# A transformer block's operations recorded first and given out by the kernel's own planner

## The chip, the core and the metric

The kernel runs on one core of one Trainium2 chip. The metric is the device time of one execution in microseconds. TensorE (PE) multiplies, VectorE (DVE) and ScalarE (ACT) work on elements, SyncE (SP) issues most loads, and GpSimd (POOL) issues loads that add into their destination. Each of these engines has a queue of its own; work is handed over between engines by semaphores.

## The reference

One layer of a streaming encoder on 256 tokens with 2048 features, all in float32:

```python
x = x + 0.5 * swiglu(rms_norm(x, ffn1_norm), ffn1_w_up, ffn1_w_down)       # 2048 -> 2 x 5632 -> 2048
proj = rms_norm(x, mix_norm) @ w_in                                        # q, f, i, g, x_b, gate_b, gates
y_a = rms_norm(hgrn2_chunked(q, f, i, lb), hgrn_norm) * silu(g)            # 8 heads of 128
y_b = rglru_branch(x_b, gate_b, conv_w, conv_b, lru_wa, ...)               # conv(4), gates, linear scan, gelu
x = x + (sigmoid(gate_a) * (y_a @ w_branch_a) + sigmoid(gate_b) * (y_b @ w_branch_b)) @ w_out
x = x + cross_attention(rms_norm(x, xattn_norm), rms_norm(mem, mem_norm), wq, wkv, wo)   # 4 heads, 256 memory tokens
x = x + 0.5 * swiglu(rms_norm(x, ffn2_norm), ffn2_w_up, ffn2_w_down)
return rms_norm(x, final_norm)
```

HGRN2 is a gated linear recurrence per head, S_t = diag(f_t) S_(t-1) + (1 - f_t) v_t, read out with q_t. RG-LRU is a first-order recurrence per feature.

## The kernel before

The weights, some 450 MB, are read once, in tiles of 1 MB (128 partitions x 2048). Each tile goes through the same stages: SyncE loads it into `raw` (3 buffers); ScalarE copies it to `h`, rounded to the format TensorE takes (3 buffers); VectorE subtracts `h` from `raw` and leaves the rest in `l` (3 buffers); TensorE multiplies with `h` and `l`, and adds the products in PSUM, which has 8 banks of 128x512. `split` (lines 120 and 121) makes `h` and `l`. The activations are kept as a high and a low part too, so that one product takes three matmuls: high by high, low by high, high by low.

The feed-forward blocks go over 11 groups of 512 hidden columns. A group takes 8 tiles of the gate and up weights; the tiles are "plain", "mixed" or "fast". A fast tile goes through seven instead of eight products, for which VectorE forms four differences first (`td`, lines 213 to 215) and splits them too (`th`, `tl`). For some mixed tiles ("added") the low part is made by a load of GpSimd that adds into `l`. After a group the hidden values are transposed (line 491), and tiles of the down weights follow. `three` (lines 451 to 454) issues the matmuls of one tile. The temporary tiles `td`, `tl`, `ev` and `junk` share a pool `wide` of three buffers.

The mixer and the attention go over their tiles by `product` (lines 231 and 235: weights stationary) or `rows_product` (lines 252 to 255: activations stationary). The recurrences run beside them: `hgrn` and `lru` are generators that stand in a list `side`, and `pump(2)` takes up to two steps of them after each tile. A step of HGRN is some small matmuls on TensorE (lines 768 and 788, tiles of 32 or 16 columns), then a few products on VectorE.

A list `plan` holds all weight tiles in the order of use; `weights` prepares each of them up to two ahead of its use. The program text fixes a priority, and the framework's own scheduler puts the instructions of each engine in order from that priority and from durations of its own. The kernel overrules it at four places: SyncE, ScalarE and VectorE keep the written order for the first eight tiles; the rows' norm, the LRU parameters and the side work are held behind an operation of the main work by `issue_after`.

Of the kernel before, what the change touches and what calls it, by code (L numbers as in the profile page):

```python
# [2 lines left out]

# [4 lines left out]

F32 = mybir.dt.float32
F32R = mybir.dt.float32r  # L10
ACT = mybir.ActivationFunctionType
ALU = mybir.AluOpType
# [45 lines left out]
    return out + [("down", NG - 2, 2, c, b) for c in range(4) for b in (NG - 2, NG - 1)]  # L58


@with_exitstack
def block_kernel(ctx: ExitStack, tc: tile.TileContext, xT, xin, memT, vec, gfin, bgate, lruw, wu1, wd1, win, wv,
                 wg, wab, wout, wq, wk, wvm, wo, wu2, wd2, out_):
    nc = tc.nc
    pe, dve, act, sp = nc.tensor, nc.vector, nc.scalar, nc.sync

    def pool(name, bufs, **kw):
        return ctx.enter_context(tc.tile_pool(name=name, bufs=bufs, **kw))

    const = pool("const", 1)  # L70
    rawp = pool("raw", 3)
# [5 lines left out]
    scoped = {}  # L77

    @contextmanager
    def scope(**pools):  # L80
        with ExitStack() as inner:
            for name, bufs in pools.items():
                scoped[name] = inner.enter_context(tc.tile_pool(name=name, bufs=bufs, reuse_waits="tile"))
            yield
            scoped.clear()

    def slot(dt=F32, name="slot"):
        return slots.tile([P, 1024], dt, name=name, tag="slot")
# [71 lines left out]

    head, rest = [], {}
    planned = count()
    in_turn = ExitStack()

    def weights(*key):
        while plan and len(ahead) < 2:
            i = next(planned)
            k, src, kind = plan.pop(0)
            if i == 0:
                in_turn.enter_context(tc.manual_schedule(engines={sp.engine, act.engine, dve.engine}))  # L170
            if i < len(head):
                head[i]()
            if plan and plan[0][2] == "added":
                begun.append(begin_added(plan[0][1]))
            ahead.append((k, prepare(src, kind, 4 if i < 4 else 1)))
# [10 lines left out]
    def begin_added(src):  # L186

        raw = scoped["own"].tile([P, 2048], F32, name="own", tag="own")
        l = lp.tile([P, 2048], F32R, name="l", tag="l")
        sp.dma_start(raw, src)  # L190
        act.activation(l, raw, ACT.Copy, scale=-1.0)
        nc.gpsimd.dma_start(l, raw, accum_op=ALU.add)
        return raw, l

    def prepare(src, kind, cuts=1):
# [271 lines left out]
    def ffn(name, pairs, sq, then, begin=(), sums=(), rstds=()):  # L467
# [3 lines left out]
        order = orders[name]  # L471
# [7 lines left out]
        rstd = None  # L479
# [26 lines left out]

        for at, e in enumerate(order):
            w = weights(name, *e)
            kind = e[0]
            following = order[at + 1][0] if at + 1 < len(order) else None  # L510
            if kind != "down":
                g, p = e[1:]
                fast = kind == "fast"
                products = []
                for i, (a, b, n) in enumerate(PRODUCTS[kind]):
                    u = uses[g, n]
                    if u[0] == (p, i):
                        accs[n] = bank()
                    own, less = pairs[p]
                    products.append((accs[n], part(own, a, P) if a >= 0 else part(less, -1 - a, P), part(w[b // 4] if fast else w, b % 4, 512),  # L520
                                     u[0] == (p, i), u[-1] == (p, i)))
                three(products)
                last = at + 1 == len(order) or order[at + 1][1] != g or following == "down"
                ends = kind != "plain" and uses[g, 0][-1][0] == p
                if ends or last:
                    if ends or kind == "plain":
                        ev = scoped["wide"].tile([P, 2048], F32, name="ev", tag="wide")
                        e0, e1, e2, e3 = (ev[:, i * 512:(i + 1) * 512] for i in range(4))
                        if rstds:
                            rstd = rstds[0]  # L530
                        if rstd is None:
                            with tc.issue_after(done["high"]):
                                rstd = sq.rstd_tokens()
                if ends:
                    act.activation(e0, accs[0], ACT.Copy)
                    dve.tensor_tensor(out=e1, in0=accs[5], in1=e0, op=ALU.add)
                    dve.tensor_tensor(out=e2, in0=accs[4], in1=e1, op=ALU.add)
                if last:
                    if kind == "plain":
                        activate(e0, accs[0], accs[1], 0)  # L540
                        activate(e3, accs[3], accs[2], 1)
                    else:
                        for o, n, x in ((e0, 1, e0), (e1, 3, e1), (e1, 2, e1)):
                            dve.tensor_tensor(out=o, in0=accs[n], in1=x, op=ALU.add)
                        activate(e0, e0, e1, 0)
                        for o, n, x in ((e3, 6, e2), (e2, 3, e2)):
                            dve.tensor_tensor(out=o, in0=accs[n], in1=x, op=ALU.add)
                        activate(e3, e3, e2, 1)
                    late.append((4 if g else 2, lambda g=g, hid=(e0, e3): turn(g, hid)))
            else:  # L550
                first, n, c, block = e[1:]
                if block == first:
                    accs["down"] = [bank(), bank()]
                for t in range(2):
                    products = []
                    for k in range(4):
                        a = hids[2 * block + k // 2][:, k % 2 * 512:][:, :512]
                        products.append((accs["down"][t], (a[:, t * P:][:, :P], a[:, T + t * P:][:, :P]),
                                         part(w, k, 512), block == first and k == 0, block == first + n - 1 and k == 3))
                    three(products)  # L560
                    if block == first + n - 1:
                        o = xt[c][:, t * 512:(t + 1) * 512]
                        done["residual"] = dve.scalar_tensor_tensor(out=o, in0=accs["down"][t], scalar=0.5, in1=o,
                                                                    op0=ALU.mult, op1=ALU.add).ins
                        if block == NG - 1:
# [84 lines left out]
    def to_mix(c, t):  # L650
        sq2.add(c, [t])
        if t == 0:
            return
        if c == 0:
            with tc.issue_after(done["residual"]):
                parameters()
        if c == 2:
            root_ready(xt[c])
        if c < 3:
            normed(xs2, c, "mix_norm")  # L660
        else:
            late2.append(lambda: normed(xs2, c, "mix_norm"))
# [23 lines left out]
    v = [scoped["extra"].tile([P, 1024], F32, name=f"v{t}", tag="extra") for t in range(2)]  # L686
# [65 lines left out]
    def hgrn(hf):  # L752
        q, f = Q[hf], F[hf]
# [3 lines left out]
        S = scoped["scores"].tile([P, 3 * 512], F32, name="S", tag="S")  # L757
# [16 lines left out]
        nc.gpsimd.memset(S[:, :1024], 0.0)  # L774
        yield
        dve.tensor_tensor(out=q, in0=q, in1=f, op=ALU.mult)
        yield True
# [2 lines left out]
        for li, n in enumerate(LEVELS):  # L780
            acc = bank()
            if n >= 32:
                for g in range(2):
                    for h in range(4):
                        i = g * 4 + h
                        for a in range(0, P, 2 * n):
                            s = g * P + a
                            pe.matmul(acc[a:a + n, i * n:(i + 1) * n], kv[:, h, s:s + n], qv[:, h, s + n:s + 2 * n],
                                      start=True, stop=True)
# [18 lines left out]
            for t, side_of, by in ((q, 1, 0), (kk, 0, 1)):  # L808
                o = t.rearrange("p (j two n) -> p j two n", two=2, n=n)[:, :, side_of]
# [13 lines left out]
        for pair in range(2):  # L823
            os, squares = [], []
            for z in range(2):
                h = pair * 2 + z
                c = (hf * 4 + h) * P
                o = bank()
# [3 lines left out]
                s = t1("osq")  # L832
# [197 lines left out]
    for g in range(4):  # L1030
# [65 lines left out]

    with scope(**FFN_POOLS):
        ffn("ffn2", pairs2, sq4, to_out, late, sums2)


def _layout(inputs):
# [90 lines left out]
```

## Time and profile before

| what | us |
|---|---|
| time, median of the runs (2442.12 to 2442.47) | 2442.3 |
| time of the profiled execution | 2442.24 |
| its span, from the first to the last instruction | 2440.5 |
| TensorE busy | 2430.0 |
| weight loads of TensorE, beside its matmuls | 2033.8 |
| VectorE busy | 1892.8 |
| ScalarE busy | 1390.8 |
| GpSimd busy | 28.3 |

The span begins with the first instruction of the program and ends with its last. A matmul's record ends some time after the next one has begun, so TensorE's busy time is the union of overlapping records. Idle time of an engine is put down to what ended it. The core read 472.07 MB at 194 GB/s over the span, and TensorE's granted clock was 0.999 of full speed.

### The profile page before, as it was taken

Reading aid. Unit: us, or ns where it says so; the run is one execution under the profiler, and the core shown is the slowest. Engines: PE = TensorE matmul, PEld = TensorE weight load, DVE = VectorE, ACT = ScalarE, POOL = GpSimd, SP = SyncE. Lnnn points to the kernel's source line nnn. Section 1 sums busy time; section 2 is a strip of 40 time slices with the busy share of each in tenths; the row PEclk is TensorE's granted clock in tenths of the full one; section 3 lists DMA queues with packets and bytes.
Section 4 is the critical chain, followed back from the end, with each engine's and each line's share of the span. In section 5 each row is a group of like instructions: output and inputs, shape, how many; then the busy total and the mean of one; then the engine's idle time right before and its main releaser. Section 6 shows DMA issues by size and latency. Waiting matters only on the chain.

```text
span 2440.5 us, 30183 instructions
## 1 busy us (share of the span) xinstructions
PE 2430.0 (100%) x12250; PEld 2033.8 (83%) x12250; DVE 1892.8 (78%) x2016; ACT 1390.8 (57%) x1398; POOL 28.3 (1%) x36
## 2 busy tenths in 40 slices
PE   9999999999999999999999999999999999999998
PEld 8888888888888888888888888888888888888887
DVE  6999999999765757577565676556589999999995
ACT  8566666666554454477435554555555666666664
POOL 0000000000000000000000000000000000000000
PEclk9999999999999999999999999999999999999999
DMA  8557777677555545445555555544555677777763
GB/s 296 207 204 243 255 234 236 234 241 239 200 181 192 180 173 179 176 171 217 191 189 186 206 196 190 190 173 155 189 191 185 232 238 234 234 239 241 237 216 151
DMA packets 75020, 507.59 MB, mean 208 GB/s; under 512 B 8320, under 2 KB 8576, under 8 KB 15232
## 3 DMA queue, kind: packets, MB, share of 16 engines
q1 hardware_dynamic: 69840, 473.06, 53.3%
q0 software_dynamic: 4320, 31.46, 6.7%
q8 instruction: 96, 1.57, 0.2%
q10 hardware_dynamic: 720, 1.13, 0.1%
q14 instruction: 44, 0.36, 0.0%
HBM read 472.07 MB, written 2.10 MB: 194 GB/s over the span
## 4 chain that ended last, share of the span: by engine, by line
PE 97%; DVE 1%; ACT 1%; DMA 1%; issue 0%; SPq 0%; ACTq 0%; DVEq 0%
PE acc L451 18%; PE acc L454 18%; PE acc L452 18%; PE acc L231 11%; PE acc L252 8%; PE acc L253 8%; PE acc L255 8%; PE acc L235 6%; PE acc L491 1%; PE acc L391 1%; ACT h L120 0%; PE acc L768 0%; DVE l L121 0%; DMA xf<-xT 0%; PE acc L1051 0%; PE acc L1006 0%
## 5 line engine op out<-in xcount | busy, mean ns | idle before, releaser
L121 DVE TENSOR_TENSOR l<-raw,h 128x2048 fp32r<-128x2048 f32 (+2 forms) x422 | 877.9, 2087 | 364.8 <-ACT h L120 354.7
L120 ACT ACTIVATE h<-raw 128x2048 fp32r<-128x2048 f32 (+2 forms) x422 | 736.7, 1752 | 615.1 <-PE acc L253 206.2
L451 PE MATMUL acc<-h,xh 128*128 128x512 f32 x1280 | 499.0, 391 | 0.4 <-ACT h L120 0.3
L452 PE MATMUL acc<-h,xl 128*128 128x512 f32 x1280 | 496.9, 389 | 0.0
L120 ACT ACTIVATE h<-td 128x1024 fp32r<-128x1024 f32 x224 | 229.7, 1056 | 177.0 <-PE acc L452 130.8
L252 PE MATMUL acc<-h,ops 128*128 128x512 f32 x832 | 326.9, 393 | 0.0
L253 PE MATMUL acc<-h,ops 128*128 128x512 f32 x832 | 324.3, 390 | 0.0
L121 DVE TENSOR_TENSOR tl<-td,h 128x1024 fp32r<-128x1024 f32 x224 | 267.4, 1220 | 31.6 <-ACT h L120 29.0
L451 PEld LDWEIGHTS acc<-h,xh 128*128 128x128 f32 x1280 | 240.3, 188 | 53.2 <-ACT h L120 3.4
L452 PEld LDWEIGHTS acc<-h,xl 128*128 128x128 f32 x1280 | 240.3, 188 | 49.4
L231 PE MATMUL acc<-ops,h 128*128 128x512 f32 x1152 | 277.9, 393 | 0.2
L451 PE MATMUL acc<-h,hidop 128*128 128x512 f32 x704 | 275.7, 392 | 0.0
L452 PE MATMUL acc<-h,hidop 128*128 128x512 f32 x704 | 274.3, 390 | 0.0
L231 PEld LDWEIGHTS acc<-ops,h 128*128 128x128 f32 x1152 | 211.9, 188 | 42.8 <-DVE ops L292 0.9
L454 PE MATMUL acc<-l,xh 128*128 128x512 f32 x832 | 218.3, 389 | 0.0
L255 PE MATMUL acc<-l,ops 128*128 128x512 f32 x832 | 206.1, 390 | 0.0
L454 PE MATMUL acc<-l,hidop 128*128 128x512 f32 x704 | 188.3, 389 | 0.0
L255 PEld LDWEIGHTS acc<-l,ops 128*128 128x128 f32 x832 | 156.2, 188 | 32.4
L454 PEld LDWEIGHTS acc<-l,xh 128*128 128x128 f32 x832 | 156.0, 188 | 32.5
L252 PEld LDWEIGHTS acc<-h,ops 128*128 128x128 f32 x832 | 156.3, 188 | 32.3
L253 PEld LDWEIGHTS acc<-h,ops 128*128 128x128 f32 x832 | 156.3, 188 | 31.6
L454 PEld LDWEIGHTS acc<-l,hidop 128*128 128x128 f32 x704 | 132.2, 188 | 27.5
(220 smaller groups left out, 2347.9 us busy)
## 6 DMA issues: line engine op xcount, KB each, us to landing
raw<-wu SPq DMA_DIRECT2D x142, 1024.0 KB, 4.8
raw<-wd SPq DMA_DIRECT2D x88, 1024.0 KB, 4.8
raw<-win SPq DMA_DIRECT2D x40, 1024.0 KB, 4.8
raw<-wg SPq DMA_DIRECT2D x32, 1024.0 KB, 4.8
own<-wu SPq DMA_DIRECT2D x30, 1024.0 KB, 5.4
l<-own POOLq DMA_DIRECT2D x30, 1024.0 KB, 7.7
raw<-wab SPq DMA_DIRECT2D x16, 1024.0 KB, 4.8
raw<-wout SPq DMA_DIRECT2D x16, 1024.0 KB, 4.8
```

Of the source, the lines that this page charges most:

```text
L120: done["high"] = act.activation(h, raw, ACT.Copy).ins
L121: dve.tensor_tensor(out=l, in0=raw, in1=h.bitcast(F32), op=ALU.subtract)
L231: pe.matmul(acc, h[:, k * P:(k + 1) * P], xs[k], start=k == 0, stop=False)
L235: done["product"] = pe.matmul(acc[:, :T], l[:, k * P:(k + 1) * P], xs[k][:, :T], start=False, stop=k == KT - 1).ins
L252: pe.matmul(accs[t], x[:, t * P:][:, :P], h[j], start=first and j == 0, stop=False)
L253: pe.matmul(accs[t], x[:, T + t * P:][:, :P], h[j], start=False, stop=False)
L255: done["product"] = pe.matmul(accs[t], x[:, t * P:][:, :P], l[j], start=False, stop=last and j == 3).ins
L391: pe.transpose(accs[m // 2][:, m % 2 * T + t * P:][:, :P], tile[:, t * 512 + m * P:][:, :P], ident)
L451: pe.matmul(acc, ah, bh, start=start, stop=False)
L452: pe.matmul(acc, al, bh, start=False, stop=False)
L454: pe.matmul(acc, ah, bl, start=False, stop=stop)
L491: pe.transpose(acc[:, z * T + t * P:][:, :P], hid[t][:, (2 * y + z) * P:][:, :P], ident)
```

## The change

The functions of the kernel no longer call the engines. They call stand-ins that record each operation with its tiles; the body of the kernel, its loops and the operations stay as they are. At the end `flow.emit()` works out an order for all engines in a simulated run with durations that are written in the kernel, and issues every operation in that order, under a mode in which the framework keeps the given order on all engines. The four places that overruled the framework's scheduler are gone.

- `record` notes for every operation whom it must follow: the writer of what it reads, and readers and writers of what it overwrites. PSUM is tracked by bank, other tiles by 32 columns.
- `price` gives it a duration by engine and columns: a matmul 0.0134 us plus a 2400th of a microsecond per column above 128 columns, fixed values below, VectorE 1.042 ns a column plus 0.07 us, ScalarE 0.838 ns a column plus 0.095 us, a load 2.9 us per MB plus 1.9 us.
- `nominal` gives it a place in time: the sum of TensorE's durations recorded before it.
- `aims` gives it a due time: for TensorE its nominal time, for the others the earliest due time of what follows less its own duration and a lag; a successor can pull a TensorE operation earlier too.
- `arrange` runs the engines event by event: a free engine takes, among the operations that are ready, the one with the earliest due time. Nothing runs whose nominal time lies more than 30 us ahead of TensorE. `Ring` hands out buffers: with up to 8 of them in the recorded order alone, with 24 also out of order while more than six are free. It is done three times, since the due times take up which buffers follow one another.
- `emit` names every buffer's place and issues.

```diff
+class Ring:
...
+        self.spare = bufs if bufs <= 8 else bufs // 4
...
+    def when(self, op):
+
+        if not self.free or self.takers[self.head] is not op and len(self.free) <= self.spare:
+            return 1e18
+        return min(self.free)[0]
...
+LAG = {"PE": 0.24, "DVE": 0.15, "ACT": 0.16, "POOL": 0.16, "SP": 0.1}
+AHEAD, BACKLOG = 30, 3
+TABLES = {ACT.Silu, ACT.Sigmoid, ACT.Sqrt, ACT.Exp, ACT.Gelu_apprx_tanh}
...
+    def price(self, op):
+        q, kw = op.queue.name, op.kw
+        n = op.out.cells.size if op.out is not None else 0
+        op.table, op.moved, op.busy = None, 0, 0.0
+        if op.method == "dma_start":
+            v = op.out if op.out is not None else op.args[1]
+            op.moved = v.cells.size * 512 / 2 ** 20 * (5.2 if "accum_op" in kw else 2.9)
+            op.busy = 0.9 if q == "POOL" else 0.06
+        elif q == "PE":
+            op.busy = n / 2400 + 0.0134 if n > 128 else 0.108 if n == 128 else 0.058 if n == 64 else 0.04
+        elif q == "DVE":
+            n = max(n, kw["in_"].cells.size) if op.method == "tensor_reduce" else n
+            per = {"reciprocal": 6.2, "tensor_tensor_scan": 2.2}.get(op.method, 1.042)
+            op.busy = n * per / 1000 + 0.07
+        elif q == "ACT":
+            op.busy = n * 0.838e-3 + 0.095 + (0.1 if "accum_out" in kw else 0)
+            op.table = op.args[2] if op.args[2] in TABLES else None
...
+    def nominal(self):
+        t = 0.0
+        for op in self.ops:
+            op.nominal = t
+            if op.queue.name == "PE":
+                t += op.busy
+
+    def aims(self, order):
+        for op in self.ops:
+            op.due = op.nominal if op.queue.name == "PE" or not op.after else 1e9
+        for op in reversed(order):
+            for s in op.after:
+                lag = op.spent if op.deps is not None and s.deps.get(op, True) is not None else 0
+                op.due = min(op.due, s.due - lag)
...
+            best, soon = None, 1e18
+            for op in cand[e]:
+                r = op.ready
+                if op.scope is not None and any(live[:op.scope]) and any(x.ring.pool.scope is not None for x in op.takes):
+                    continue
+                for x in op.takes:
+                    r = max(r, x.ring.when(op))
+                if op.nominal > reached + AHEAD:
+                    r = 1e18
+                if op.moved:
+                    r = max(r, dma - BACKLOG)
+                if r <= t + 1e-9:
+                    if best is None or op.due < best.due:
+                        best = op
+                else:
+                    soon = min(soon, r)
...
+            if op.table is not None and op.table != table:
+                table = op.table
+                busy += 1.3
...
+        self.nominal()
+        for _ in range(3):
+            self.arrange()
...
+            outer.enter_context(tc.manual_schedule())
+            for op in self.sequence:
...
+                for x in op.takes:
+                    x.at = x.ring.pool.at.tile(x.shape, x.dt, name=x.name, tag=f"{x.ring.tag}{x.index}")
+                getattr(op.queue.real, op.method)(*map(real, op.args), **{k: real(v) for k, v in op.kw.items()})
...
+    flow = Flow(tc)
+    pe, dve, act, sp, gps = flow.queues
+    pool = flow.pool
...
-            if i == 0:
-                in_turn.enter_context(tc.manual_schedule(engines={sp.engine, act.engine, dve.engine}))
...
-            if i == 7:
-                in_turn.close()
...
-                            with tc.issue_after(done["high"]):
-                                rstd = sq.rstd_tokens()
+                            rstd = sq.rstd_tokens()
...
-            with tc.issue_after(done["residual"]):
-                parameters()
+            parameters()
...
-                with tc.issue_after(done["product"]):
-                    n -= n if next(side[0]) else 1
+                n -= n if next(side[0]) else 1
...
+    flow.emit()
```

More of the change, by code (lines that the diff above doesn't have):

```diff
@@ L2 @@
 from itertools import count
+import numpy as np
 import concourse.bass as bass
@@ L6 @@
 from concourse import mybir
-from concourse._compat import with_exitstack
 F32 = mybir.dt.float32
@@ L58, in ffn_order, with __init__, then, __getitem__ @@
     return out + [("down", NG - 2, 2, c, b) for c in range(4) for b in (NG - 2, NG - 1)]
-@with_exitstack
-def block_kernel(ctx: ExitStack, tc: tile.TileContext, xT, xin, memT, vec, gfin, bgate, lruw, wu1, wd1, win, wv,
+class View:
+    def __init__(self, tile, cells, steps=()):
+        self.tile, self.cells, self.steps = tile, cells, steps
+    def then(self, cells, f):
+        return View(self.tile, cells, self.steps + (f,))
+    def __getitem__(self, key):
+        key = key if isinstance(key, tuple) else (key,)
+        return self.then(self.cells[key[1:]], lambda v: v[key if len(key) > 1 else key[0]])
+    def rearrange(self, pattern, **sizes):
+        names = pattern.split("(")[1].split(")")[0].split()
+        return self.then(self.cells.reshape([sizes.get(n, -1) for n in names]),
+                         lambda v: v.rearrange(pattern, **sizes))
+    def bitcast(self, dt):
+        return self.then(self.cells, lambda v: v.bitcast(dt))
+    def broadcast_to(self, shape):
+        return self.then(np.broadcast_to(self.cells, shape[1:]), lambda v: v.broadcast_to(shape))
+    def real(self):
+        v = self.tile.at
+        for f in self.steps:
+            v = f(v)
+        return v
@@ new lines, with __init__, reset, take @@
+class Buffer(View):
+    def __init__(self, ring, shape, dt, name):
+        grain = shape[1] if "space" in ring.pool.kw else 1 if shape[1] <= 128 else 32
+        super().__init__(self, np.arange(shape[1]) // grain)
+        self.ring, self.shape, self.dt, self.name = ring, shape, dt, name
+        self.at = self.index = None
+        n = -(-shape[1] // grain)
+        self.writer, self.readers = [None] * n, [set() for _ in range(n)]
+        self.users = []
+        self.left = 0
+class Ring:
+    def __init__(self, pool, tag, bufs):
+        self.pool, self.tag, self.bufs = pool, tag, bufs
+        self.takers = []
+        self.spare = bufs if bufs <= 8 else bufs // 4
+        self.reset()
+    def reset(self):
+        self.free = [(0.0, i, None) for i in range(self.bufs)]
+        self.head, self.taken = 0, set()
+    def when(self, op):
+        if not self.free or self.takers[self.head] is not op and len(self.free) <= self.spare:
+            return 1e18
+        return min(self.free)[0]
+    def take(self, op):
+        f = min(self.free)
+        self.free.remove(f)
+        self.taken.add(op)
+        while self.head < len(self.takers) and self.takers[self.head] in self.taken:
+            self.head += 1
+        return f
@@ new lines, with __init__, tile @@
+class Pool:
+    def __init__(self, flow, name, bufs, scope, **kw):
+        self.flow, self.name, self.bufs, self.scope, self.kw = flow, name, bufs, scope, kw
+        self.rings = {}
+        self.at = None
+    def tile(self, shape, dt, name, tag=None, bufs=None):
+        tag = tag or name
+        if tag not in self.rings:
+            self.rings[tag] = Ring(self, tag, bufs or self.bufs)
+        return Buffer(self.rings[tag], shape, dt, name)
+class Op:
+    def __init__(self, i, queue, method, args, kw):
+        self.i, self.queue, self.method, self.args, self.kw = i, queue, method, args, kw
+        self.deps, self.after, self.takes, self.frees = {}, [], [], []
+        self.ins = self
+        self.scope = None
@@ L63, in block_kernel @@
+def block_kernel(tc: tile.TileContext, xT, xin, memT, vec, gfin, bgate, lruw, wu1, wd1, win, wv,
                  wg, wab, wout, wq, wk, wvm, wo, wu2, wd2, out_):
[L64 to L68, printed above, removed]
+    flow = Flow(tc)
+    pe, dve, act, sp, gps = flow.queues
+    pool = flow.pool
     const = pool("const", 1)
@@ L80, in scope @@
     def scope(**pools):
[L81 to L85, printed above, removed]
+        for name, bufs in pools.items():
+            scoped[name] = pool(name, bufs, flow.scopes)
+        flow.scopes += 1
+        yield
+        scoped.clear()
     def slot(dt=F32, name="slot"):
@@ L162, in block_kernel @@
     planned = count()
-    in_turn = ExitStack()
     def weights(*key):
@@ L191, in begin_added @@
         act.activation(l, raw, ACT.Copy, scale=-1.0)
-        nc.gpsimd.dma_start(l, raw, accum_op=ALU.add)
+        gps.dma_start(l, raw, accum_op=ALU.add)
         return raw, l
@@ L773, in hgrn @@
                           in1=col("eye", 0, 32)[:, None, :].broadcast_to([P, 8, 32]), op=ALU.mult)
-        nc.gpsimd.memset(S[:, :1024], 0.0)
+        gps.memset(S[:, :1024], 0.0)
         yield
```

181 lines of the change are left out of this document (added).

## The prediction

> **What bounds the kernel now.** I read the page's busy times and its chain first, then who TensorE waited for.
>
> ```profile
> span 2440.5 us, 30183 instructions
> PE 2430.0 (100%) x12250; PEld 2033.8 (83%) x12250; DVE 1892.8 (78%) x2016; ACT 1390.8 (57%) x1398; POOL 28.3 (1%) x36
> PE 97%; DVE 1%; ACT 1%; DMA 1%; issue 0%; SPq 0%; ACTq 0%; DVEq 0%
> PE warm L109 <- DVE ones L106: 1.1, 1, 1.1
> PE acc L451 <- ACT h L120: 0.3, 1, 0.3
> ```
>
> TensorE is the bound from end to end: the chain is 97% its own work, and the only wait in the body that the profile shows is one of 0.3 us. A busy share near 100% still hides small losses, because one matmul's record overlaps the next. So I looked at when matmuls start. The next rows are the timeline: start, duration, instruction. The first real matmul, the two rough places of the ramp, one insertion of small work, and the last matmuls:
>
> ```profile
> 6.99 0.48 PE L451 MATMUL acc<-h,xh 128*128 128x512 f32 x1
> ...
> 27.73 1.29 PE L454 MATMUL acc<-l,xh 128*128 128x512 f32 x5
> 29.31 0.50 PE L451 MATMUL acc<-h,xh 128*128 128x512 f32 x1 [0.28 <-ACT h L120]
> 29.65 0.39 PE L452 MATMUL acc<-h,xl 128*128 128x512 f32 x1
> 29.88 0.40 PE L451 MATMUL acc<-h,xh 128*128 128x512 f32 x1
> ...
> 74.01 0.39 PE L452 MATMUL acc<-h,xl 128*128 128x512 f32 x1
> 74.40 0.50 PE L451 MATMUL acc<-h,xh 128*128 128x512 f32 x1
> 74.74 0.40 PE L452 MATMUL acc<-h,xl 128*128 128x512 f32 x1
> ...
> 76.14 0.64 PE L454 MATMUL acc<-tl,xh 128*128 128x512 f32 x2
> 76.92 0.50 PE L451 MATMUL acc<-h,xh 128*128 128x512 f32 x1
> 77.25 0.40 PE L452 MATMUL acc<-h,xl 128*128 128x512 f32 x1
> ...
> 845.51 1.07 PE L255 MATMUL acc<-l,ops 128*128 128x512 f32 x4
> 846.51 0.74 PE L768 MATMUL acc<-silu,k 128*32 128x16 f32 x64
> 847.18 0.50 PE L252 MATMUL acc<-h,ops 128*128 128x512 f32 x1
> 847.51 0.40 PE L253 MATMUL acc<-h,ops 128*128 128x512 f32 x1
> ...
> 2430.67 1.07 PE L454 MATMUL acc<-l,hidop 128*128 128x512 f32 x4
> ```
>
> From 29.65 to 29.88 a 128x512 matmul takes 0.23 us of the stream. Against that pace the first rough place loses 29.31 - (27.73 + 5 x 0.23) = 0.4 us and 0.1 after it; the second 0.16 + 0.11; the third 0.32 + 0.10. Together 1.2 us. An insertion of HGRN's small matmuls loses about 0.1 going in, 0.1 in its own last step and 0.1 coming out (847.18 to 847.51 is 0.33): 0.3 us. The program makes 28 such insertions (12 for L768, 4 for L788, 2 for L819, 4 for L829, 4 for L838, 2 for L872), which makes 28 x 0.3 = 8.4 us, an estimate. Everything an order can win is in these few microseconds and in the two ends: 6.99 us before the first real matmul, 2440.5 - 2431.7 = 8.8 us after the last.
>
> Then the stretches, which say how much room the other engines have (busy us of TensorE, of its weight loads, VectorE, ScalarE and GpSimd, each with its instructions in brackets; clock, share and GB/s of the transfers), then when the mixer's first product starts on the chain, and who waited for whom:
>
> ```profile
> 6.00:80.00 74.00, 73.58 (x328) 59.03 (x328) 59.99 (x86) 57.34 (x87) 0.00 (x0) 1.00 0.74 272
> 80.00:200.00 120.00, 120.00 (x537) 98.89 (x536) 118.44 (x120) 70.81 (x60) 1.00 (x1) 1.00 0.61 221
> 200.00:600.00 400.00, 400.00 (x1795) 331.81 (x1794) 371.05 (x361) 247.30 (x200) 11.28 (x13) 1.00 0.73 237
> 702.00:1120.00 418.00, 417.88 (x2961) 357.55 (x2960) 269.02 (x313) 222.57 (x238) 1.91 (x2) 1.00 0.51 183
> 1790.00:2420.00 630.00, 630.00 (x2822) 521.92 (x2821) 572.17 (x543) 375.83 (x308) 13.01 (x15) 1.00 0.67 224
> ...
> 702.88 2.72 PE acc L231 x12
> ...
> DVE l L121 <- ACT h L120: 354.7, 222, 4.6
> ACT h L120 <- PE acc L452: 298.9, 194, 3.9
> ACT h L120 <- PE acc L253: 206.2, 70, 4.4
> ```
>
> VectorE (the third busy time) is nearly as full as TensorE in both feed-forward blocks (371 of 400 us, 118 of 120) and has a third of its time free in the mixer. Where it idles, it waits for ScalarE's high halves, and ScalarE waits for TensorE to give a buffer of h back (298.9 + 206.2 us): the producers run ahead until the three buffers are full. That is the slack a new order works with.
>
> **The change part by part.** The profiled execution took 2442.24 us, its span and 1.8 us around it; the median of the runs is 2442.3, so the sum needs no shift.
>
> TensorE's order: for TensorE a due time is the operation's place in the recorded order, unless a successor pulls it earlier. The recording follows the old program text, rings of up to 8 buffers (all 8 PSUM banks, h, l, raw) are given out in recorded order, and matmuls into one bank are chained. So the products keep their order; what can move is small work: the transposes and HGRN/LRU pieces go in when they are ready by the planner's clock, perhaps in the middle of a product. The trace of before has no split piece; bounds are 28 x 0.3 = 8.4 us more if each is cut in two, and 4.2 us less if half of them merge. I take three more cuts, +0.9: most pieces wait for one producer, only LRU's four blocks become ready one by one.
>
> The start: ScalarE runs two small operations of the LRU parameters before the first operand.
>
> ```profile
> 4.31 0.21 ACT L631 ACTIVATE par<-vt 128x8 f32<-128x8 f32 x1 [1.63 <-DMA vt<-vec]
> 4.55 0.21 ACT L632 ACTIVATE par<-par 128x8 f32<-128x8 f32 x1
> 4.66 0.89 ACT L414 ACTIVATE xg<-xf,vt 128x256 f32<-128x256 f32 x2
> 5.59 0.63 ACT L120 ACTIVATE xh<-xg 128x512 fp32r<-128x512 f32 x1
> 6.12 2.45 ACT L120 ACTIVATE h<-raw 128x512 fp32r<-128x512 f32 x4
> 6.86 2.49 DVE L121 TENSOR_TENSOR l<-raw,h 128x512 fp32r<-128x512 f32 x4
> ```
>
> They are recorded at the end of the first feed-forward block, and the planner holds back all that lies over 30 us ahead. They leave the start, and xg can begin at 4.31 instead of 4.66: up to 0.35 us earlier, nothing if the data of xf land later than that. I take -0.3. Late next is the quarter of h at 6.12.
>
> The ramp: the 1.2 us of gaps above lie at ScalarE's h and VectorE's tl. Earliest due first would do urgent splits ahead of the operand sums (they follow TensorE's use of them). Bounds 0 and -1.2; half, -0.6.
>
> VectorE, ScalarE, SyncE and GpSimd in the steady stretches: every operation stays, so their busy times stay; a new order costs nothing as long as two products lie ready. Cover gone, it costs what the first rival says. The removed holds (rstd behind the high half, parameters behind the residual, side work behind the product) let these operations go earlier on their queues, past one 2.3 us split at most, which the buffers cover; the parameters' exponential costs a table load anywhere:
>
> ```profile
> L121 DVE TENSOR_TENSOR l<-raw,h 128x2048 fp32r<-128x2048 f32 x294 | 671.4, 2289 | 341.1 <-ACT h L120 338.6 <-ACT lo L264 2.2
> 2423.39 1.28 ACT L372 ACT_TABLE_LOAD   x1
> 2424.68 0.20 ACT L372 ACTIVATE root<-root 128x1 f32<-128x1 f32 x1
> ```
>
> Table loads: the planner prices a switch at 1.3 us and does not group by table. Twenty more would be 26 us of ScalarE, against 418 - 222.6 = 195 us free in the mixer's first stretch: 0 on the path. [...]
>
> Transfers: same number, same queues. A load leaves SyncE when its buffer is free; the planner's limit of 3 us of backlog orders them and delays nothing on the chip. 0; the end behind the last matmul is a chain of eight dependent steps whose order is given: 0, within 0.5 either way.
>
> Sum: +0.9 - 0.3 - 0.6 = 0.0, so 2442 us.
>
> **The rivals.** (a) Slower, a producer's queue blocked in the feed-forward blocks. VectorE takes its instructions in order; where the planner lets it begin something a little before it is ready on the chip, everything behind waits. A group of gate columns lasts (702.88 - 6.99) / 11 = 63 us, and VectorE is idle 28.95 of 400 us there, 4.6 us a group. From more than 4.6 us lost per group on, TensorE pays the rest, in 22 groups: half a microsecond over gives +11 (2453), one gives +22 (2464). For it: 93 to 99% busy, and the planner's durations are a formula. Against it: ScalarE's 505 us of waiting for TensorE says that the buffers are mostly full. [...]
>
> (b) Slower, TensorE's small pieces cut in two or more: +8.4, 2450.6. The planner charges 0.04 us for a 16-column matmul, where 32 of them (64 records) took 0.67 us, so it believes these pieces take twice as long, and nothing for the 0.3 us of a switch. That speaks for it; the single producer per piece speaks against.
>
> (c) Faster: the ramp smooth (-1.2), the start (-0.35), half of the insertions merged (-4.2): 2436.5. Against it: in the recording two steps of HGRN lie a product or two apart, and a later due time keeps them there.
>
> (d) No change in effect, the planner rebuilds the old order: 2442.2. Recorded order as the due time of TensorE speaks for it.
>
> [...]
>
> **How the numbers follow.** The forecast (steady stretches covered, small terms cancelling) has 0.38, (d) 0.12: both lie within 0.2%, 2437.4 to 2447.2, which is about what a measurement of this kernel can tell from no change. (a) has 0.20 and (b) 0.16; (c) 0.13 and (e) 0.01. So faster 0.14, same 0.50, slower 0.36. The range leaves out (e) and the far end of (c) below, and of (a) what lies over one microsecond a group above: 2435 to 2466. The likeliest case's own range is 2439 to 2446, its terms at their ends and half of the bound on cuts.
>
> **What would show it.** Right: TensorE's waits stay under 2 us, VectorE's busy time of 200 to 600 us stays near 371, the first real matmul starts near 6.7, the ramp's three gaps shrink, and the small pieces of L768 still come 64 records at a time. (a) would show as waits of TensorE for VectorE's l or tl at the same place of every group, and VectorE idle on something other than h; (b) as L768 or L872 in groups of fewer records between product matmuls. Wrong would also be a start of the second block or of the mixer at which TensorE waits several microseconds for a scoped buffer, since a scope opens only when the last operation of the one before is given out.

## The result and the profile after

The changed kernel takes 2582.1 us in the median (2577.6 to 2585.92) against 2442.2 us before: 1.0572 times as long, with an interval of 1.0552 to 1.0592. That is 140 us more. The forecast was no change, 2442 us, in a range of 2435 to 2466.

The page of the changed kernel, its head and its chain, then who TensorE waited for (line 409 stands for every operation now, because one line issues them all):

```profile
span 2575.8 us, 30258 instructions
PE 2560.5 (99%) x12250; PEld 2076.0 (81%) x12250; DVE 1899.1 (74%) x2016; ACT 1397.8 (54%) x1403; POOL 28.3 (1%) x36
PE 96%; DVE 2%; issue 1%; ACT 1%; DMA 0%; ACTq 0%; DVEq 0%
PE acc L409 <- DVE ops L409: 3.1, 2, 1.6
PE warm L409 <- DVE ones L409: 1.1, 1, 1.1
PE acc L409 <- DVE hidop L409: 1.0, 3, 0.6
PE acc L409 <- ACT S L409: 0.5, 1, 0.5
```

TensorE is still the bound, with the same 12250 matmuls. It waits for others 5.7 us in all, the 1.1 us of the first instruction included. So 130 us of new time are not waits: TensorE is counted as busy in them. VectorE's and ScalarE's busy times have grown by 6 and 7 us only. The stretches tell where it is (columns as in the prediction); the feed-forward block first, then the part of the mixer in which the recurrences run:

```profile
200.00:600.00 400.00, 400.00 (x1793) 330.83 (x1792) 371.26 (x360) 248.94 (x200) 11.28 (x13) 1.00 0.73 237
...
720.00:1130.00 410.00, 409.50 (x2343) 291.74 (x2342) 186.37 (x226) 125.07 (x135) 0.95 (x1) 0.99 0.35 126
```

In the feed-forward block nothing has changed: 1793 matmuls in 400 us, where it was 1795, and VectorE is busy 371.26 us, where it was 371.05. In the mixer TensorE gets 2343 matmuls done in 410 us, where before 2961 fitted into 418; VectorE and ScalarE have less to do than before, so they aren't what holds it. The timeline of TensorE in that stretch, its weight loads (PEld) with it:

```profile
840.16 0.40 PE L409 MATMUL acc<-ops,l 128*128 128x256 f32 x2
840.49 0.14 PEld L409 LDWEIGHTS acc<-silu,k 128*32 128x32 f32 x2
840.49 0.24 PE L409 MATMUL acc<-silu,k 128*32 128x16 f32 x2
840.65 0.19 PEld L409 LDWEIGHTS acc<-ops,h 128*128 128x128 f32 x1
840.65 0.50 PE L409 MATMUL acc<-ops,h 128*128 128x512 f32 x1
841.08 0.14 PEld L409 LDWEIGHTS acc<-silu,k 128*32 128x32 f32 x2 [0.25 <-issue]
841.08 0.23 PE L409 MATMUL acc<-silu,k 128*32 128x16 f32 x2
841.25 0.19 PEld L409 LDWEIGHTS acc<-ops,l 128*128 128x128 f32 x1
841.25 0.39 PE L409 MATMUL acc<-ops,l 128*128 128x256 f32 x1
```

In the kernel before, 64 records of HGRN's 16-column matmuls stood together. Here each of them (two records) stands alone between two product matmuls. From 840.49 to 841.08 one small matmul and one 128x512 matmul take 0.59 us; whole, the first would take 0.02 us (0.67 us for 64 records) and the second 0.23. A cut costs 0.34 us. The rows say why: each weight load begins together with its own matmul. The product's load of 0.19 us at 840.65 runs in the open, and the product's record is 0.50 us long instead of 0.40. The two loads in the open, 0.14 and 0.19 us, make 0.33 us, about the cut. Across these small tiles the rows show no load ahead of its matmul; among products the trace does: the 1408 loads for the matmuls of `h` by `hidop` begin 0.22 us ahead of them in the median.

That this is a matter of the small tiles and not of any change of shape is seen where transposes stand alone between product matmuls of the same kernel:

```profile
648.06 0.39 PE L409 MATMUL acc<-h,hidop 128*128 128x512 f32 x1
648.06 0.14 PEld L409 LDWEIGHTS acc<-vt,ev 128*128 128x128 f32 x1
648.29 0.27 PE L409 MATMUL acc<-vt,ev 128*128 128x128 f32 x1
648.29 0.19 PEld L409 LDWEIGHTS acc<-l,hidop 128*128 128x128 f32 x1
648.32 0.47 PE L409 MATMUL acc<-l,hidop 128*128 128x512 f32 x1
648.40 0.19 PEld L409 LDWEIGHTS acc<-h,hidop 128*128 128x128 f32 x1
648.63 0.39 PE L409 MATMUL acc<-h,hidop 128*128 128x512 f32 x1
```

The load of the transpose stands at 648.06, a matmul ahead, and transpose and product take 648.63 - 648.29 = 0.34 us together, what they take apart (0.11 + 0.23). The 84 transposes of this trace that stand alone between two 128x512 products take 0.34 us with the product too, on average. These cuts are free. Nor is it that HGRN's matmuls leave two records each. Those of its last level have 128 stationary columns instead of 32, read the same tiles, and stand alone too:

```profile
1151.52 0.42 PEld L409 LDWEIGHTS acc<-silu,k 128*128 128x128 f32 x2
1151.75 0.38 PE L409 MATMUL acc<-silu,k 128*128 128x128 f32 x2
1151.89 0.48 PE L409 MATMUL acc<-l,ops 128*128 128x512 f32 x1
1152.20 0.27 PE L409 MATMUL acc<-silu,k 128*128 128x128 f32 x1
```

Their loads stand ahead, and the pair takes 1152.20 - 1151.75 = 0.45 us, what it takes apart (2 x 0.11 + 0.23). Both their stationary and their moving columns are more, so this doesn't separate the two. One matmul does in part: `ones` by `ss`, 128 stationary columns and a single moving one, stands alone at 1592.07. Its load begins at 1591.84, a matmul ahead, and its cut costs about 0.2 us (1592.07 to 1592.52 for it and a product of 0.23). So in this trace the load that doesn't come ahead goes with the narrow stationary tile, while a part of the 0.35 us may come from the few moving columns.

Counted over the whole trace by what a matmul reads, HGRN's matmuls come in 390 stretches instead of 26 (those with 32 or 64 stationary columns in 363 instead of 16), the transposes in 186 instead of 48, and between neighbouring products there are 1415 changes between 512 and 256 columns instead of 254.

**Where the cuts come from.** The planner takes the ready operation with the earliest due time. `aims` pulls a due time earlier than the recorded place so that what follows can be in time: by `op.spent`, which is the operation's duration and a lag, for TensorE 0.24 us. In the planner this lag stands for the time until another engine sees the result. But `aims` also takes it between two TensorE operations that follow one another in one PSUM bank, where the trace of before shows no wait: from 702.88 on, 12 matmuls of one product take 2.72 us, 0.227 us each. A column product is a chain of 32 matmuls in one bank: 16 x 0.227 + 16 x 0.120 = 5.6 us of work at the paces of that trace, with 31 links from one matmul to the next; the first is due 31 x 0.24 = 7.4 us too early. HGRN's chain of 32 small matmuls has 0.28 us from one due time to the next, for 0.04 us of priced work. Two or three such chains now overlap in due time, one with a step of 0.36 or 0.47 us, the other with 0.28. Taken by due time, they come out alternately. That is the theory (A) which the runs test. Its rivals were: (B) the planner's order of VectorE and ScalarE blocks their queues, the prediction's rival (a); (C) it is the products alternating that costs; (D) the too high price of small matmuls makes the planner cut them, as the prediction's rival (b) held.

### The profile page after: what moved, and what is told of

The parts are those of the page before. It is cut to its first block, busy times and chain, and to the rows that moved or that the text cites. A ratio compares the mean times of both kernels' runs of the same rounds, so it can differ in the third digit from the quotient of the medians.

```text
span 2575.8 us, 30258 instructions
## 1 busy us (share of the span) xinstructions
PE 2560.5 (99%) x12250; PEld 2076.0 (81%) x12250; DVE 1899.1 (74%) x2016; ACT 1397.8 (54%) x1403; POOL 28.3 (1%) x36
## 3 DMA queue, kind: packets, MB, share of 16 engines
q8 instruction: 96, 1.57, 0.2%
## 4 chain that ended last, share of the span: by engine, by line
PE 96%; DVE 2%; issue 1%; ACT 1%; DMA 0%; ACTq 0%; DVEq 0%
PE acc L409 96%; DVE l L409 1%; DVE ev L409 1%; DVE x L409 0%; DVE td L409 0%; ACT h L409 0%; PE warm L409 0%; DMA raw<-wu 0%; DVE tl L409 0%; ACT x L409 0%; DVE hidop L409 0%; DVE ops L409 0%; ACT junk L409 0%; ACT S L409 0%; ACTq L409 0%
## 5 line engine op out<-in xcount | busy, mean ns | idle before, releaser
L409 PE MATMUL acc<-h,xl 128*128 128x512 f32 x1280 | 458.2, 389 | 0.0
L409 PE MATMUL acc<-h,hidop 128*128 128x512 f32 x1408 | 448.7, 393 | 0.0
L409 PE MATMUL acc<-h,ops 128*128 128x512 f32 x1664 | 425.3, 397 | 0.0
L409 PE MATMUL acc<-ops,h 128*128 128x512 f32 x1152 | 406.8, 411 | 3.1 <-DVE ops L409 3.1
L409 PEld LDWEIGHTS acc<-h,hidop 128*128 128x128 f32 x1408 | 262.4, 188 | 52.6
L409 PE MATMUL acc<-ops,l 128*128 128x256 f32 x1152 | 289.7, 298 | 0.0
L409 PE MATMUL acc<-l,hidop 128*128 128x512 f32 x704 | 266.1, 393 | 0.0
L409 PE MATMUL acc<-l,ops 128*128 128x512 f32 x832 | 235.4, 399 | 0.0
L409 PEld LDWEIGHTS acc<-ops,l 128*128 128x128 f32 x1152 | 207.3, 189 | 17.6
L409 DVE TENSOR_TENSOR td<-raw,td 128x512 f32<-128x512 f32 x224 | 154.0, 688 | 3.6
```

Of the source, the lines that this page charges most:

```text
L409: getattr(op.queue.real, op.method)(*map(real, op.args), **{k: real(v) for k, v in op.kw.items()})
```

## The experiments

**The lag out of the chain.** One line in `aims`, the rest of the planner untouched:

```diff
                 lag = op.spent if op.deps is not None and s.deps.get(op, True) is not None else 0
+                if lag and s.queue is op.queue and op.queue.name == "PE":
+                    lag = op.busy
                 op.due = min(op.due, s.due - lag)
```

> Between two TensorE operations the due time is pulled earlier by the first one's duration alone, without the 0.24 us of lag; all else as in the changed kernel. Theory A (the lag in the chain cuts the small pieces into fragments between product matmuls, and each cut costs about 0.3 us): HGRN's pieces come whole again, 26 of them as before, and the time falls to 2438 to 2450. Theory B (the planner's order of VectorE and ScalarE blocks their queues): that order is still the planner's, so the time stays over 2560.

Measured: 2438.76 us in the median (2438.46 to 2439.51), 0.9986 times the kernel before (0.9977 to 0.9996). HGRN comes in 26 pieces again. The whole loss is gone, and a small gain is left, though VectorE, ScalarE and the queues are still in the planner's order: theory B falls. The head of its page, TensorE's only wait, and two stretches:

```profile
span 2436.9 us, 30205 instructions
PE 2427.7 (100%) x12250; PEld 2034.9 (84%) x12250; DVE 1902.0 (78%) x2016; ACT 1395.5 (57%) x1403; POOL 28.3 (1%) x36
PE warm L411 <- DVE ones L411: 1.1, 1, 1.1
0.00:80.00 80.00, 78.94 (x360) 66.35 (x361) 66.89 (x93) 61.54 (x93) 0.20 (x4) 1.00 0.76 276
720.00:1130.00 410.00, 410.00 (x2901) 350.75 (x2901) 264.83 (x300) 219.44 (x229) 0.95 (x1) 1.00 0.51 182
```

2901 matmuls in the 410 us in which the changed kernel got 2343 done. The first 80 us hold 360; in the kernel before they hold 349:

```profile
0.00:80.00 80.00, 78.53 (x349) 63.97 (x350) 60.15 (x87) 60.45 (x93) 0.20 (x4) 1.00 0.74 267
```

Eleven matmuls of 0.227 us are 2.5 us: the ramp is where the planner is better than the old order. VectorE has 66.9 us done in that stretch instead of 60.2.

**Whole pieces, products still alternating.** Due times as in the changed kernel, but a small piece is not left once begun (after a matmul of up to 256 columns that begins a sum of its own, TensorE goes on in the same bank while it can):

```diff
-        table = None
+        table = last = None
...
+            if e == "PE" and last is not None and last.out.cells.size <= 256 and last.kw.get("start") is not False:
+                for op in cand[e]:
+                    if op.out.tile is last.out.tile and op.ready <= t + 1e-9:
+                        best = op
+            if e == "PE":
+                last = best
             op = best
```

> Due times as in the changed kernel, but once TensorE has begun a small piece it goes on with the next matmul into the same bank if that is ready. Products still alternate with one another (1626 changes between 512 and 256 columns, 1415 in the changed kernel, 254 before), HGRN comes in 30 pieces. Theory A: 2450 to 2465, the alternation of products costs some 6 ns a change. Theory C (alternating products are what costs): stays over 2550. Theory B: stays over 2560.

Measured: 2451.2 us (1.0035, 1.0019 to 1.005). Products alternate as much as in the changed kernel, and this costs 2451.2 - 2438.8 = 12.4 us with all that comes with it. In its profiled execution TensorE waits 3.8 us in the body, where the run with the lag out has no wait; the first real matmul comes at 7.60 us instead of 6.52; and the clock is halved for 3.41 us. Theory C falls: alternating products explain at most a tenth.

**The lag between small matmuls alone.**

```diff
+                if lag and s.queue is op.queue and op.queue.name == "PE" and op.out.cells.size > 64:
+                    lag = op.busy
```

> The lag is kept in the due times between matmuls of up to 64 columns alone; products come in the old order (248 changes of size), HGRN in 290 pieces. Theory A: 264 cuts more than before at 0.32 us make 84 us, 2515 to 2545. Theory C: about 2445. Theory B: over 2560.

Measured: 2531.2 us (1.0364, 1.0343 to 1.0385). Products in order, HGRN in 290 pieces: 92.4 us over the run with the lag out. That is 264 cuts at 0.35 us, and the timeline of this run shows that period directly, from 831.69 to 832.29:

```profile
831.69 0.14 PEld L411 LDWEIGHTS acc<-silu,k 128*32 128x32 f32 x2 [0.24 <-issue]
831.69 0.23 PE L411 MATMUL acc<-silu,k 128*32 128x16 f32 x2
831.86 0.19 PEld L411 LDWEIGHTS acc<-ops,h 128*128 128x128 f32 x1
831.86 0.50 PE L411 MATMUL acc<-ops,h 128*128 128x512 f32 x1
832.29 0.14 PEld L411 LDWEIGHTS acc<-silu,k 128*32 128x32 f32 x2 [0.24 <-issue]
```

0.60 us for what takes 0.25 when it stands apart.

**Half of the lag.**

```diff
+                if lag and s.queue is op.queue and op.queue.name == "PE":
+                    lag = op.busy + 0.5 * LAG["PE"]
```

> Half of the lag between TensorE operations, 0.12 us: HGRN in 300 pieces, 1336 changes of size. Theory A: 274 cuts at 0.32 us and some 15 us of the rest make 2530 to 2560, under the changed kernel. Theory B: unchanged, about 2580.

Measured: 2559.7 us (1.048, 1.0459 to 1.0501), at the upper end of what was expected. Of its 274 more pieces 261 are of matmuls with 32 or 64 stationary columns. With the alternations that makes 2438.8 + 261 x 0.35 + 12.4 = 2543; 17 us are left over. The granted clock (the column behind the last bracket) tells whose they are:

```profile
780.00:860.00 80.00, 80.00 (x510) 58.61 (x509) 38.56 (x52) 25.76 (x29) 0.00 (x0) 0.95 0.36 127
860.00:940.00 80.00, 80.00 (x461) 54.81 (x462) 31.06 (x39) 22.71 (x26) 0.00 (x0) 0.90 0.31 110
...
1000.00:1060.00 60.00, 60.00 (x361) 41.04 (x360) 21.39 (x31) 13.14 (x11) 0.00 (x0) 0.83 0.31 112
1060.00:1110.00 50.00, 50.00 (x286) 35.39 (x286) 17.94 (x23) 12.66 (x13) 0.00 (x0) 0.83 0.29 98
```

80 x 0.05 + 80 x 0.10 + 60 x 0.17 + 50 x 0.17 = 31 us of clock were withheld while alternating matmuls ran. Not all of it costs time: in the changed kernel a 256-column product and a small matmul take 0.48 us at full clock (1100.57 to 1101.05) and 0.73 at half (1102.22 to 1102.95), not 0.96; 17 of 31 us would account for the rest. The changed kernel has the same in one place, 1100 to 1110 us, at 0.59, and once more for 3.41 us at 1494, after a wait of 1.57 us. That the clock causes the difference is read from these rows; no run held it constant.

**No pull at all.** A TensorE operation is due at its recorded place:

```diff
+                if op.queue.name == "PE":
+                    continue
                 op.due = min(op.due, s.due - lag)
```

> A TensorE operation is due at its recorded place alone, no successor pulls it earlier. HGRN in 26 pieces, LRU in 10, 254 changes of size. Theory A (the chain's lag, and not the planner as such): 2437 to 2441, like the run with the chain at its duration alone (2438.8). If some of the pulling is needed: over 2442, with waits of TensorE.

Measured: 2439.5 us (0.9988, 0.9979 to 0.9998), 0.7 us over the run with the lag out, inside both intervals. So the pulling is not needed; only the wrong lag in it did harm.

**TensorE in the recorded order, waits included.**

```diff
-        done = 0
+        done = pe_done = 0
+        recorded = [op for op in ops if op.queue.name == "PE"] + [None]
...
             for op in cand[e]:
+                if e == "PE" and op is not recorded[pe_done]:
+                    continue
                 r = op.ready
...
             cand[e].remove(op)
+            pe_done += e == "PE"
```

> TensorE must take its operations in the recorded order, and waits where the next one is not ready; the other engines are given out by the planner. LRU comes in 2 pieces, 42 transposing pieces. Theory A: 2437 to 2442, the freedom of choice on TensorE is worth little. If that freedom hides waits: over 2444, with TensorE waiting in the mixer.

Measured: 2475.2 us (1.0136, 1.0121 to 1.0151). The second expectation came true. Its waits:

```profile
PE acc L413 <- DVE hidop L413: 9.4, 4, 4.1
PE acc L413 <- ACT i L413: 6.8, 4, 2.8
PE acc L413 <- DVE p L413: 2.9, 1, 2.9
PE acc L413 <- ACT r L413: 2.3, 4, 0.6
PE acc L413 <- DVE x L413: 2.0, 3, 0.7
...
165.26:172.09 6.83, 6.05 (x17) 4.89 (x18) 5.74 (x8) 2.08 (x2) 0.00 (x0) 0.50 0.56 210
```

They add up to 23 us of the 36. The longest, 4.1 us twice, are four transposes that start 0.06 us after VectorE has read the four before them (`hidop`); then come LRU's blocks (`i` and `r`, 6.8 and 2.3 us), where the planner, which tracks PSUM by bank, lets the next matmul write one half only after ScalarE has read the other. The other 13 us go with the clock: TensorE is busy 2442.2 us here and 2427.7 with the lag out, 14.5 us more, and its clock is halved at the end of the long waits and just after (the last row; that wait ends at 166.04). All such stretches before the last matmul add up to 30.7 us, of which half, 15 us, is withheld (the mean clock of this execution is 0.992). So taking what is ready is worth some 36 us against the order as written. Against the kernel before nothing follows from this, since its order is the framework's and not the written one.

**Lower prices of small matmuls**, once with the lag out of the chain, once in the changed kernel:

```diff
-            op.busy = n / 2400 + 0.0134 if n > 128 else 0.108 if n == 128 else 0.058 if n == 64 else 0.04
+            op.busy = n / 2400 + 0.0134 if n > 128 else 0.108 if n == 128 else 0.03 if n == 64 else 0.014
```

> The chain at its duration alone as before in the run of 2438.8, and small matmuls priced at 0.014 us up to 32 columns and 0.03 at 64, in place of 0.04 and 0.058. Same number of pieces. Theory A: 2437.5 to 2440, the price of small matmuls matters little.

> The changed kernel, its lag in the chain kept, with these lower prices of small matmuls alone. HGRN in 370 pieces, 1427 changes of size. Theory A: 344 cuts at 0.345 us and 12 us of alternating products on 2438.8 make 2570, 2560 to 2585. Theory D (the too high price of small matmuls makes the planner cut them, as the prediction held): under 2480.

Measured: 2438.9 us (0.9985, 0.9976 to 0.9995) with the lag out, the same as with the old prices; 2583.7 us (1.0578, 1.0557 to 1.0599) with the lag kept. HGRN is in 370 pieces there, so right prices save 20 of 390 pieces and no time: the 20 x 0.35 = 7 us may be given back by the clock, which is halved for 37.5 us in this trace (mean 0.992) and for 13.7 us in the changed kernel's (mean 0.996). Theory D falls.

## Why the prediction was wrong

**TensorE as the bound, and 0.3 us for an insertion.** Right for TensorE, and right for the matmuls of L768 and L788 with 32 and 64 stationary columns: a cut costs 0.35 us by the run with the lag on small matmuls alone (92.4 us over 264 more pieces of HGRN). It is not right for all 28 insertions. Those of L819, L829, L838 and L872 have 128 stationary columns, and in the changed kernel such cuts cost next to nothing (0.45 us for a pair that takes 0.45 apart, above). Nor was the trace of before without a split piece: L872 stands in four places there, 14 and 2 records for each half.

**"TensorE's order", +0.9.** This is the step that failed. I wrote that a due time is the recorded place "unless a successor pulls it earlier" and that "the products keep their order", and took three more cuts with a bound of 28. I never worked the pull out along a chain in one bank, though the two figures it needs stood in the diff: 0.24 us of lag and 31 links are 7.4 us, more than a product's whole 5.6 us. Working it out gives overlapping chains. Measured: 364 cuts more, 347 of them at 32 or 64 stationary columns, at 0.35 us 121 us; alternating products with their waits 12 us; the better ramp and end -3.5 us. This makes 2442.2 + 121 + 12 - 3.5 = 2572. Halved clock may hold the 10 us left to the median: 13.7 us of it withhold 7 us in the profiled execution of 2577.6 us, and of the four executions the two at a granted clock of 0.996 took 2577.6 and 2579.7 us, those at 0.993 and 0.992 took 2584.5 and 2585.9. No run held the clock constant.

**The bound of rival (b).** The mechanism was its mechanism, pieces cut among product matmuls. Its size was not: I halved each piece, as if a piece could only be interrupted once. A planner that picks one operation at a time cuts down to single matmuls, so the bound was the 432 HGRN matmuls of 32 and 64 stationary columns at 0.35 us, 150 us, and the range should have reached there. What I held for it, the price of 0.04 us, had hardly a part in it (20 of 390 pieces).

**Rival (a), a producer's queue blocked.** It didn't happen: VectorE's 371 us in the 400 us from 200 to 600 are the same, as the row shows, and with the lag out the planner's order of the other engines is not slower. That VectorE holds back what stands behind a waiting instruction does show in the trace of before: it is idle 3.14 us up to 16.42, waiting for xh, while the first sums xs, whose xg was done by 9.49, begin at 22.99.

**The start, -0.3.** The two parameter operations did leave it: xg begins at 4.54 us instead of 4.66. But the first real matmul comes at 7.02 (6.99 before), because the 16 warming matmuls were still running:

```profile
1.06 6.21 PE L409 MATMUL warm<-ones 128*128 128x128 f32 x32 [1.06 <-DVE ones L409]
7.02 0.71 PE L409 MATMUL acc<-h,xh 128*128 128x512 f32 x2
```

In the run with the lag out they took 5.61 us and the first real matmul came at 6.52. What is late next at the start was the warming, not the quarter of h, as I had it; so it was in the kernel before, where h is ready at 6.74 and the last warming matmul starts at 6.96. The warming matmuls start 0.21 us apart at first and 0.11 later, and that change comes at about 6 us before and after, at about 4.8 in the run with the lag out. Nothing in the runs ties it to the planner's order; by these traces the start is in part luck.

**The ramp, -0.6.** Right in sign, too small: 2.5 us with the start's half microsecond, seen in the run with the lag out. I had added up three gaps; several of 0.1 us each around 60 us lay beside them.

**Steady stretches at nothing, table loads, transfers.** Right, as far as the unchanged feed-forward rows and the run with the lag out show it; ScalarE has five table loads more (37 instead of 32, at 1.28 us each) and 7 us more of busy time, and TensorE's waits name none of them. The parameters' exponentials did not each cost a load: in the trace of before L624 has one, L632 at 4.55 none. **The end, within 0.5.** Just outside: with the lag out the last matmuls begin at 2427.66 and take 1.07 us, which leaves 2436.9 - 2428.7 = 8.2 us instead of 8.8; in the changed kernel it is 9.4 us. **Rival (e)**, a far faster kernel, had a chance of 0.01; no run shows one, and the shortest median is 2438.76 us.

**What would have shown it** named L768 in groups of fewer records. That is what the trace shows.

## What to carry to other kernels

Work a planner's due times out by hand along its longest chain before trusting its order: here a lag of 0.24 us meant for another engine was taken between neighbours on one queue that begin 0.227 us apart without a wait, and it multiplied by the 31 links of the chain. Before moving small matmuls among large ones, look at whether the large ones' weight loads still stand ahead of their matmuls; where they didn't here, a cut cost 0.35 us. A busy share near 100% says nothing of this (99% in the changed kernel); the number of matmuls done in a stretch of fixed length does (2343 against 2901 in 410 us).

## What was not expected of the hardware

A single small matmul of 32 stationary columns between two products costs 0.35 us, while a single transpose, or a matmul of 128 stationary columns by the same function, costs nothing measurable in the same kernel (0.34 and 0.45 us with their products, as much as apart). All need other weights than the product; the trace shows the loads of the wide tiles ahead and the small tile's load together with its matmul. No run changed the width of the tile alone.

TensorE's clock was lowered while TensorE was busy without a pause. In the changed kernel:

```profile
1100.57 0.23 PE L409 MATMUL acc<-silu,k 128*32 128x16 f32 x2
1100.74 0.38 PE L409 MATMUL acc<-ops,l 128*128 128x256 f32 x1
1101.05 0.24 PE L409 MATMUL acc<-silu,k 128*32 128x16 f32 x4
...
1100.00:1110.00 10.00, 10.00 (x52) 6.44 (x52) 4.04 (x6) 0.38 (x1) 0.00 (x0) 0.59 0.31 107
...
1101.73:1111.97 10.24, 10.24 (x45) 6.81 (x44) 4.67 (x8) 0.38 (x1) 0.00 (x0) 0.50 0.41 142
...
1102.44 0.58 PE L409 MATMUL acc<-ops,l 128*128 128x256 f32 x1
```

Its busy time there is 10.00 of 10 us, the clock is halved from 1101.73 to 1111.97, and the same 128x256 matmul takes 0.58 us instead of 0.38. The pattern of this place is a 256-column product matmul and one small matmul, 0.48 us a pair before the clock falls (1100.57 to 1101.05), of which the product takes 0.12 us by its pace. In the run with the lag on small matmuls alone, whose rows above show 512 columns with each small matmul, the clock stayed at 1.00 over the whole stretch:

```profile
700.00:1200.00 500.00, 500.00 (x2915) 380.57 (x2915) 266.79 (x309) 213.64 (x225) 1.26 (x2) 1.00 0.42 148
```

That it is this share which decides is a guess from these two patterns, and the traces of before and of the changed kernel bear it out. From about 6 us on, where the warming matmuls quicken, and up to the last matmul, each stretch at one clock in the changed kernel's trace lasts a whole number of 3.413 us (10.24, 382.29 and 3.41 among them). Cut both traces into steps of that length, and add up the matmuls that fall in each step at full clock, at their usual paces: 0.227 us for 512 columns, 0.120 for 256, 0.109 for a transpose, 0.01 for a small one. By this estimate the two steps of the changed kernel after which the clock fell were filled to 0.31 and 0.39, and of its 743 others at full clock none under 0.37; in the trace of before none of 710 was filled under 0.60, and the clock stayed at 1.00. No run changed this share alone.

The profile shows no wait of TensorE from 1090 to 1115 us, and none longer than 1.6 us in the body of the changed kernel.
